# Weight sums of a seven-product unit: formed by accumulating transfers instead of VectorE, from quarter tiles

## The chip, the cores and the metric

The kernel runs on one core of a Trainium2 chip. The metric is the device time of one execution in microseconds. The engines are TensorE (PE in the profile), VectorE (DVE), ScalarE (ACT), GpSimd (POOL) and SyncE (SP); SP issues the loads from HBM, GpSimd issues a few transfers of its own queue.

## The reference

Two layers of a decoder trunk over 528 positions (16 meta and 512), with D = 1024 and FF = 2816, in fp32. Each layer is an FFN with a gate, a norm, a mixer, a norm, a second such FFN and a norm; the mixer is a short gated convolution in the first layer and forgetting attention in the second, whose K and V come from the end of the first.

```python
def swiglu(x, wg, wu, wd):
    return (jax.nn.silu(x @ wg) * (x @ wu)) @ wd
...
    for l in range(DEPTH):
        h = layer_norm(DEEPNORM_ALPHA * h + 0.5 * swiglu(h, ffn1_wg[l], ffn1_wu[l], ffn1_wd[l]),
                       ln_gain[l, 0], ln_bias[l, 0])
        if l < N_A:
            mix = short_conv(h, conv_w_in[l], conv_w[l], conv_w_out[l])
        else:
            j = l - N_A
            mix = forgetting_attention(h, attn_w_q[j], attn_w_o[j], k_sh, v_sh, c_sh)
        h = layer_norm(DEEPNORM_ALPHA * h + mix, ln_gain[l, 1], ln_bias[l, 1])
        h = layer_norm(DEEPNORM_ALPHA * h + 0.5 * swiglu(h, ffn2_wg[l], ffn2_wu[l], ffn2_wd[l]),
                       ln_gain[l, 2], ln_bias[l, 2])
        if l == N_A - 1:
            k_sh, v_sh, c_sh = shared_kv(h, kv_w, f_bias)
```

## The kernel before

Every fp32 matrix is used as a sum of a high and a low part. For a weight, ScalarE casts the raw tile to `wh` (L132) and VectorE subtracts to get `wl` (L134); this is `split_w`. A product is then three matmuls for one (`gemms`, L244): low times high, high times low, high times high.

The weights of gate and up (a pair `wg`, `wu`), and of K and V, are taken in **units** of 256 columns. A unit splits the 1024 rows of its weight and its 256 columns in two, so there are quarters a11, a12 (the upper rows), a21, a22 (the lower rows), each 128 x (2 matrices x 4 row blocks x 128 columns). In place of eight products of quarters it takes seven, with sums of weight quarters on the left and sums of activations (t1 to t4) on the right. The sums on the left are

- s1 = a21 + a22, s2 = s1 + a11, s3 = a11 + a21, s4 = s2 + a12 (signs are put into the activations).

In the kernel before, VectorE forms them: `s` into a tile of its own (L200), s3 in the place of a21 (L201), s2 in the place of a11 (L202), s4 in the place of a12 (L211). Each sum is then split like any weight. `Quads` holds the quarters of one unit; `Unit` holds the products p1 to p7; `run_units` sets TensorE's order: p5, p6, p7, the next unit's p1, then p4, p3, and the next unit's p2. Each product is 24 matmuls. p1 (a11), p6 (s2), p7 (s3) and p4 (a22) accumulate one after another into the same two PSUM banks (`pb`), and ScalarE copies the banks out after p1 (L544), p6 (L558) and p7 (L564); p5 (s1) and p3 (s4) go into two other banks. Where the first activations of an FFN are not ready in time for sums, its first unit is a `Direct` one: eight products of plain quarters.

There are 48 units: 11 in each of four FFNs, in chunks of 2, 3, 3 and 3, and 4 for K and V. Four are direct, so 44 form sums. After each chunk `down` multiplies the chunk's hidden rows with `wd` (`Weights`, loaded in pieces of 256 columns).

Raw weights lie in a pool of 3 tiles of 128 x 8 x 256 (L60); a unit takes two, one per half of the rows, each filled by two loads of 512 KB in runs of 1 KB. `wh` and `wl` have 5 tiles each, PSUM has 8 banks. TensorE's order is the one written out in the program. The other engines' order is made by the tile scheduler; each engine executes its queue in order, and a low part is placed right behind its cast (`behind`, L112). Among the steps around the change: `Mixed.early` (L312) prepares the left parts of a unit ahead of a norm's end; the norm's reciprocal root is a chain of small VectorE instructions (L351 to L359); `project` (calls at L1056) forms Q for some heads, for which `q_w` splits the weights.

Of the kernel before, what the change touches and what calls it, by code (L numbers as in the profile page):

```python
# [9 lines left out]
F32 = mybir.dt.float32  # L10
# [3 lines left out]
ALU = mybir.AluOpType  # L14
# [4 lines left out]
P = 128  # L19
D = 1024  # L20
KD = D // P
# [21 lines left out]
KH = KD // 2  # L43
# [3 lines left out]
def trunk_kernel(  # L47
# [7 lines left out]
    nc = tc.nc  # L55
# [15 lines left out]
    def htile(name, dtype=F32R):  # L71
        return hid.tile([P, T], dtype, tag="h", name=name)
# [38 lines left out]
    @contextmanager  # L111
    def behind(*after):  # L112


        with ExitStack() as stack:
            for ins in after or newest[-1:]:
                stack.enter_context(tc.issue_after(ins.ins))
            yield

    def split_w(src, shape, home=None):  # L120

        n = math.prod(shape)
# [12 lines left out]
        return a, b  # L135

    class Weights:


        def __init__(self, w_ap, r0, kn, c0, n):  # L140
            self.a, self.r0, self.kn, self.c0, self.n = w_ap, r0, kn, c0, n
            self.raw, self.got, self.home = {}, {}, {}

        def load(self, m):
            g = m // 2
            if g not in self.raw:
                raw = rawp.tile([P, KD, 256], F32, tag="raw", name="raw")
                self.raw[g] = raw
                c = self.c0 + g * 256
                nc.sync.dma_start(  # L150
                    raw[:, :self.kn, :],
                    self.a[self.r0:self.r0 + self.kn * P, c:c + 256].rearrange("(k p) n -> p k n", p=P))
            return self.raw[g]

        def __call__(self, m):
            if m not in self.got:
                raw = self.load(m)
                g = m - m % 2
                if self.kn <= KH:
                    src = raw[:, :self.kn, :].rearrange("p k (j n) -> p j k n", j=2)  # L160
                    wh, wl = split_w(src, (2, self.kn, P))
                    for j in range(2):
                        self.got[g + j] = wh[:, j], wl[:, j]
                else:
                    self.got[m] = split_w(
                        raw[:, :self.kn, (m - g) * P:(m - g + 1) * P], (self.kn, P), self.home.get(m))
            return self.got[m]

    class Quads:
# [1 line left out]

        def __init__(self, aps, home=None):
            self.aps, self.raws, self.got, self.home = aps, {}, {}, home

        def load(self, half):
            if half not in self.raws:
                raw = rawp.tile([P, KD, 256], F32, tag="raw", name="raw")
                raw = raw.rearrange("p (j k) n -> p j k n", j=2)  # L180
                self.raws[half] = raw
                for j, a in enumerate(self.aps):
                    nc.sync.dma_start(
                        raw[:, j], a[half * KH * P:(half + 1) * KH * P, :].rearrange(
                            "(k p) n -> p k n", p=P))
            return self.raws[half]

        def part(self, m, half):
            return self.load(half)[:, :, :, m * P:(m + 1) * P]

        def sums(self):
            if "s" in self.got:
                return
            self("a11")
            s = wp.tile([P, KD * P], F32, tag="ws", bufs=1, name="s")
            s = s.rearrange("p (j k n) -> p j k n", j=2, k=KH)
            self.got["s"] = s
            a11, a21, a22 = self.part(0, 0), self.part(1, 0), self.part(1, 1)
            with behind():
                nc.vector.tensor_tensor(s, a21, a22, ALU.add)  # L200
                nc.vector.tensor_tensor(a21, a11, a21, ALU.add)  # L201
                nc.vector.tensor_tensor(a11, a11, s, ALU.add)  # L202

        def __call__(self, name):
            if name not in self.got:
                if name[0] == "s":
                    self.sums()
                if name == "s4":
                    a12 = self.part(0, 1)
                    with behind():  # L210
                        nc.vector.tensor_tensor(a12, a12, self.part(0, 0), ALU.add)  # L211
                src = {"a11": lambda: self.part(0, 0), "a12": lambda: self.part(0, 1),
                       "a21": lambda: self.part(1, 0), "a22": lambda: self.part(1, 1), "s1": lambda: self.got["s"],
                       "s2": lambda: self.part(0, 0), "s3": lambda: self.part(1, 0),
                       "s4": lambda: self.part(0, 1)}[name]()
                self.got[name] = split_w(src, (2, KH, P), self.home)
            return self.got[name]


# [65 lines left out]
    class Mixed:  # L285
# [26 lines left out]
        def early(self):  # L312


            self.left("a11")
            self.left("a12")
            self.left.sums()

        def sums(self):

# [307 lines left out]
                nxt.p2()  # L628

    def pair_quads(wg, wu, c0, home=None):  # L630
        return Quads([a[:, c0:c0 + 256] for a in (wg, wu)], home)

    def ffn(layer, wg, wu, wd, ln, xs, to, last=None, ready=None, ahead=None):

# [58 lines left out]
    first = f1[0]  # L693
    half = D // 2
# [104 lines left out]
    def z_operands(h):  # L799
# [6 lines left out]
         Norm(0, 1, EPS, xs1), ALPHA, ahead=first_four(f2[0]))  # L806

    kv_quads = [
        Quads([kv_w[:, j * D + i * 256:j * D + (i + 1) * 256] for j in range(2)], None if i else xtile)
        for i in range(H // 2)]  # L810
    xs2 = Mixed(0, kv_quads[1])
    ffn(0, ffn2_wg[0], ffn2_wu[0], ffn2_wd[0], 2, xs1, xs2, ready=f2, ahead=first_four(kv_quads[0]))
# [353 lines left out]
```

## Time and profile before

| | |
|---|---|
| median of 3 runs | 1946.85 us (1944.77 to 1947.14) |
| the profiled execution | 1946.79 us, span 1945.0 us, mean granted clock 0.989 |
| TensorE busy | 1884.8 us, 97% |
| VectorE busy | 1404.0 us, 72% |
| ScalarE busy | 873.9 us, 45% |
| GpSimd busy | 136.7 us, 7% |
| load queue (q1) | 178510 packets, 182.74 MB, 29.3% of 16 engines |
| GpSimd's queue (q0) | 2016 packets, 5.49 MB, 0.8% |

The span is the time from the first to the last instruction; busy is the time in which an engine executes. TensorE is the engine that is nearly always busy, so what matters is where it stands still, and whom it waits for there. In the profile `pb`, `pc` and so on are PSUM banks named after the products, `wh`, `wl` the two parts of a weight, `xh`, `xl` and `hh`, `hl` those of activations, `s` the sum tile, `raw` the raw weights.

### The profile page before, as it was taken

What the parts mean: (1) busy time and instruction counts of PE and PEld (TensorE: products, weight loads), DVE (VectorE), ACT (ScalarE), POOL (GpSimd) and SP (SyncE); (2) the same over time, 40 slices, a digit from 0 to 9 for tenths busy, and PEclk for the clock granted to TensorE, in tenths of its full rate; (3) what the DMA queues carried; (4) which work ended last, traced back from release to release, by engine and by line L of the source; (5) the groups of instructions that cost most, each with busy time, mean ns of one, the idle gap of its engine ahead of it and who ended that gap; (6) DMA issues with size and microseconds to landing.
All of it is one profiled execution on the core that took longest, in us unless ns stands there. A gap on an engine that the chain in (4) does not pass through costs nothing.

```text
span 1945.0 us, 34609 instructions
## 1 busy us (share of the span) xinstructions
PE 1884.8 (97%) x14467; PEld 1820.9 (94%) x14467; DVE 1404.0 (72%) x2078; ACT 873.9 (45%) x1459; POOL 136.7 (7%) x198
## 2 busy tenths in 40 slices
PE   8899999999998999999999999999989989999997
PEld 7899999999998999999899998989988889989897
DVE  5785858674469776767887887767677787868685
ACT  5353535443335353535454543535455554535360
POOL 0000000300031000000411000000210220000000
PEclk9999999999999999999999999999989999999999
DMA  4333333232230332323224323232513203333241
GB/s 144 98 98 98 98 98 100 97 109 85 89 98 12 122 115 90 109 88 109 87 78 136 129 91 114 82 114 82 180 56 120 98 1 99 113 103 109 87 131 44
DMA packets 180681, 190.42 MB, mean 98 GB/s; under 512 B 5834, under 2 KB 174070, under 8 KB 180526
## 3 DMA queue, kind: packets, MB, share of 16 engines
q1 hardware_dynamic: 178510, 182.74, 29.3%
q0 software_dynamic: 2016, 5.49, 0.8%
q8 instruction: 113, 1.85, 0.4%
q14 instruction: 42, 0.34, 0.1%
HBM read 181.76 MB, written 6.44 MB: 97 GB/s over the span
## 4 chain that ended last, share of the span: by engine, by line
PE 84%; DVE 9%; DMA 2%; ACT 2%; POOL 1%; issue 1%; SPq 0%; DVEq 0%; ACTq 0%; POOLq 0%
PE pb L244 25%; PE pc L244 16%; PE pa L244 6%; PE pq L244 2%; PE pcc L244 2%; PE pcv L244 2%; PE pcb L244 2%; DVE wl L134 2%; DMA raw<-in_ffn_wu_dram 2%; PE psc L970 1%; PE po L1028 1%; DVE y L439 1%; POOL s L410 1%; ACT y L443 1%; POOL s L412 1%
## 5 line engine op out<-in xcount | busy, mean ns | idle before, releaser
L134 DVE TENSOR_TENSOR wl<-raw,wh 128x1024 fp32r<-128x1024 f32 (+1 forms) x440 | 522.1, 1192 | 196.5 <-ACT wh L132 185.0
L132 ACT CAST wh<-raw 128x1024 fp32r<-128x1024 f32 (+1 forms) x440 | 439.3, 1003 | 464.5 <-PE pc L244 74.9
L244 PE MATMUL pb<-xh,wl 128*128 128x264 f32 (+1 forms) x1408 | 398.1, 283 | 1.2 <-DVE wl L134 1.2
L244 PE MATMUL pb<-xh,wh 128*128 128x264 f32 (+1 forms) x1408 | 398.0, 283 | 0.0
L244 PE MATMUL pb<-xl,wh 128*128 128x264 f32 (+1 forms) x1408 | 397.8, 282 | 0.0
L244 PE MATMUL pc<-xh,wl 128*128 128x264 f32 (+1 forms) x960 | 276.4, 288 | 8.1 <-ACT xh L257 5.4
L244 PE MATMUL pc<-xl,wh 128*128 128x264 f32 (+1 forms) x960 | 276.0, 288 | 3.0 <-DVE xl L258 3.0
L244 PE MATMUL pc<-xh,wh 128*128 128x264 f32 (+1 forms) x960 | 275.1, 287 | 0.0
L244 PEld LDWEIGHTS pb<-xh,wl 128*128 128x128 f32 x1408 | 264.6, 188 | 1.6 <-issue 1.3
L244 PEld LDWEIGHTS pb<-xh,wh 128*128 128x128 f32 x1408 | 265.4, 189 | 0.0
L244 PEld LDWEIGHTS pb<-xl,wh 128*128 128x128 f32 x1408 | 264.5, 188 | 0.3
L244 PEld LDWEIGHTS pc<-xh,wl 128*128 128x128 f32 x960 | 184.2, 192 | 9.3 <-ACT xh L257 6.0
L244 PEld LDWEIGHTS pc<-xl,wh 128*128 128x128 f32 x960 | 184.2, 192 | 4.5 <-DVE xl L258 4.2
L244 PEld LDWEIGHTS pc<-xh,wh 128*128 128x128 f32 x960 | 184.7, 192 | 0.0
L244 PE MATMUL pa<-xh,wl 128*128 128x264 f32 (+1 forms) x352 | 99.6, 283 | 0.0
L244 PE MATMUL pa<-xh,wh 128*128 128x264 f32 (+1 forms) x352 | 99.5, 283 | 0.0
L244 PE MATMUL pa<-xl,wh 128*128 128x264 f32 (+1 forms) x352 | 99.4, 282 | 0.0
L132 ACT CAST wh<-s 128x1024 fp32r<-128x1024 f32 x44 | 46.0, 1046 | 49.0 <-DVE s L200 10.8
L244 PEld LDWEIGHTS pa<-xh,wh 128*128 128x128 f32 x352 | 66.3, 188 | 0.0
L244 PEld LDWEIGHTS pa<-xh,wl 128*128 128x128 f32 x352 | 66.1, 188 | 0.0
L244 PEld LDWEIGHTS pa<-xl,wh 128*128 128x128 f32 x352 | 66.1, 188 | 0.0
L200 DVE TENSOR_TENSOR s<-raw 128x1024 f32<-128x1024 f32 x44 | 54.2, 1232 | 15.5 <-DMA raw<-in_ffn_wu_dram 13.8
(1920 smaller groups left out, 4539.8 us busy)
## 6 DMA issues: line engine op xcount, KB each, us to landing
raw<-in_ffn_wg_dram SPq DMA_DIRECT2D x88, 512.0 KB, 3.9
raw<-in_ffn_wu_dram SPq DMA_DIRECT2D x88, 512.0 KB, 4.9
raw<-in_ffn_wd_dram SPq DMA_DIRECT2D x48, 768.0 KB, 4.6
raw<-in_conv_w_in_dram SPq DMA_DIRECT2D x12, 1024.0 KB, 4.9
raw<-in_ffn_wd_dram SPq DMA_DIRECT2D x16, 512.0 KB, 3.4
raw<-in_kv_w_dram SPq DMA_DIRECT2D x16, 512.0 KB, 4.6
raw<-in_conv_w_out_dram SPq DMA_DIRECT2D x4, 1024.0 KB, 5.4
raw<-in_attn_w_q_dram SPq DMA_DIRECT2D x4, 1024.0 KB, 4.8
```

The source lines that it names most:

```text
L132: nc.scalar.copy(a, src)
L134: nc.vector.tensor_tensor(b, src, a.bitcast(F32), ALU.subtract)
L200: nc.vector.tensor_tensor(s, a21, a22, ALU.add)
L244: nc.tensor.matmul(ps, lhsT=a[:, k, :], rhs=b(k), start=start and k == ks[0] and j == 0, stop=stop and k == ks[-1] and j == 2, skip_group_ ...
L410: nc.gpsimd.tensor_tensor(self.s1[h], yv[:, 0, :] if m == 1 else self.s1[h], yv[:, m, :], ALU.add)
L412: nc.gpsimd.tensor_tensor(self.s2[h], self.s2[h], sq, ALU.add)
L439: nc.vector.tensor_tensor(ym, ym, rb, ALU.mult)
L443: nc.scalar.activation(yv[:, j, :], yv[:, j, :], AF.Identity, scale=vecs[:, c:c + 1], bias=vecs[:, 48 + c:49 + c])
L970: nc.tensor.matmul(ps, lhsT=q[:, M + t * P:M + (t + 1) * P], rhs=kt[:, a:b], start=True, stop=True)
L1028: nc.tensor.matmul(po[:, q0:S], lhsT=vt[:, j * P:(j + 1) * P], rhs=pT[j // 2][:, j % 2, q0:S], start=j == 0, stop=False)
```

## The change

- Raw weights lie in 7 tiles of half the size. Each quarter of a unit has a tile of its own, filled by two loads of 256 KB (one per matrix) in runs of 512 B.
- The sums are no longer formed by VectorE, but by transfers of GpSimd's queue that read a quarter from HBM a second time and add it to what lies in a tile (`accum_op`). s1's tile gets a21 by a load, then a22 is added. Once s1 is split, a11 is added in the same tile: s2. Once s2 is split, a12 is added: s4. The tile of a11, once split, gets a21 added: s3. That is four pairs of added transfers per unit, 352 in all.
- `Weights` whose pieces have over 4 row blocks are loaded in single column blocks of 128 (runs of 512 B) rather than two at a time.
- `early` no longer forms sums; direct units load plain quarters; in the start two quarters are loaded before the rest of x.
- Q's first two batches are 2 and 3 heads, not 3 and 2.

The core of the diff:

```diff
-    rawp = ctx.enter_context(tc.tile_pool(name="rawp", bufs=3))
+    rawp = ctx.enter_context(tc.tile_pool(name="rawp", bufs=7))
...
+    def raw_tile(*shape):
+
+        raw = rawp.tile([P, KH * 2 * P], F32, tag="raw", name="raw")[:, :math.prod(shape)]
...
     class Weights:
...
+            self.step = 2 if kn <= KH else 1
...
     class Quads:
...
-            with behind():
-                nc.vector.tensor_tensor(s, a21, a22, ALU.add)
-                nc.vector.tensor_tensor(a21, a11, a21, ALU.add)
-                nc.vector.tensor_tensor(a11, a11, s, ALU.add)
+        NEXT = {"a11": ("s3", "a21"), "s1": ("s2", "a11"), "s2": ("s4", "a12")}
...
+        def move(self, engine, dst, name, **kw):
+            m, half = int(name[1]) - 1, int(name[2]) - 1
+            for j, a in enumerate(self.aps):
+                engine.dma_start(
+                    dst[:, j], a[half * KH * P:(half + 1) * KH * P, m * P:(m + 1) * P].rearrange(
+                        "(k p) n -> p k n", p=P), **kw)
+
+        def raw(self, name):
+            if name not in self.raws:
+                t = raw_tile(2, KH, P)
+                self.move(nc.sync, t, "a21" if name == "s1" else name)
+                if name == "s1":
+                    self.move(nc.gpsimd, t, "a22", accum_op=ALU.add)
+                self.raws[name] = t
+            return self.raws[name]
...
         def __call__(self, name):
             if name not in self.got:
...
+                t = self.raw(name)
+                self.got[name] = split_w(t, (2, KH, P), self.home)
+                if name in self.NEXT and not self.direct:
+                    then, part = self.NEXT[name]
+                    self.move(nc.gpsimd, t, part, accum_op=ALU.add)
+                    self.raws[then] = t
             return self.got[name]
...
             self.left("a11")
             self.left("a12")
-            self.left.sums()
...
-            first.load(0)
-    first.load(1)
+            first.raw("a11")
+            first.raw("a21")
+    first.load()
...
-    project(range(3), [0])
-    project(range(3, 5), [0])
+    project(range(2), [0])
+    project(range(2, 5), [0])
```

What this does to the order of the engines is shown at three places. First ScalarE, in the third unit of the second chunk of the first FFN; before, the rows run from the cast of s2 to the eviction of p6 (`pb_2282`, `pb_2283`).

```order
L132 CAST wh<-raw 128x1024 [waits Activation_49]
L649 ACTIVATE g<-pb_2112 128x264 [waits PE_49]
L132 CAST wh<-raw 128x1024 [waits PE_49,Activation_49]
L257 CAST hh<-g 128x528 [waits DVE_49]
L655 ACTIVATE g<-g 128x528 [waits DVE_49]
L132 CAST wh<-raw 128x1024 [waits DMAHW0_49,DMAHW1_49,PE_49,Activation_49]
L257 CAST hh<-g 128x528 [waits DVE_49]
L132 CAST wh<-raw 128x1024 [waits PE_49,Activation_49] x2
L558 COPY g<-pb_2282 128x264 [waits PE_49]
L558 COPY u<-pb_2283 128x264 [waits PE_49]
```

In the changed kernel the same stretch, from the cast of s2 to the eviction of p6 (`pb_2339`, `pb_2340`), reads as follows; DMASW are semaphores of GpSimd's queue, DMAHW those of SP's loads.

```order
L132 CAST wh<-raw 128x1024 [waits DMASW4_49,DMASW3_49,Activation_49]
L257 CAST hh<-g 128x528 [waits DVE_49]
L132 CAST wh<-raw 128x1024 [waits DMASW0_49,DMASW7_49,PE_49,Activation_49]
L654 ACTIVATE g<-g 128x528 [waits DVE_49]
L132 CAST wh<-raw 128x1024 [waits DMAHW6_49,DMAHW7_49,PE_49,Activation_49]
L257 CAST hh<-g 128x528 [waits DVE_49]
L132 CAST wh<-raw 128x1024 [waits DMAHW0_49,DMAHW1_49,PE_49,Activation_49]
L132 CAST wh<-raw 128x1024 [waits DMASW5_49,DMASW6_49,PE_49,Activation_49]
L557 COPY g<-pb_2339 128x264 [waits PE_49]
L557 COPY u<-pb_2340 128x264 [waits PE_49]
```

The sequence of casts and copies is nearly the same; s2, s3 and s4 (the rows with DMASW) now wait for transfers of GpSimd's queue, and s4's cast stands right ahead of p6's eviction, as it did before.

Second GpSimd. Before, its queue goes from the transfers of the start (L711, L859) straight to the sums of the first norm; in all FFN units it has nothing.

```order
L710 DMA vr<-in_conv_w_dram 24x128
L711 DMA fbias<-in_f_bias_dram 8x1
L859 DMA fr<-in_kv_w_dram 128x8x8
L765 MEMSET us 128x2 [waits DVE_49]
L410 TENSOR_TENSOR s_4035<-y 128x264 [waits DVE_49]
L410 TENSOR_TENSOR s_4035<-s_4035,y 128x264 [waits DVE_49,Pool_49]
```

In the changed kernel it has eight rows for each unit. Those from one unit's s3 to the next unit's read in this way; L191 is `Quads.move`, rows with DVE wait for a low part or for a free tile.

```order
L191 DMA raw<-in_ffn_wg_dram 128x4x128 [waits DMAHW6_49,DMASW7_49,DVE_49]
L191 DMA raw<-in_ffn_wu_dram 128x4x128 [waits DMAHW7_49,DMASW0_49]
L191 DMA raw<-in_ffn_wg_dram 128x4x128 [waits DMASW6_49,DMASW5_49,DMAHW4_49,DMASW1_49,DVE_49]
L191 DMA raw<-in_ffn_wu_dram 128x4x128 [waits DMAHW5_49,DMASW2_49]
L191 DMA raw<-in_ffn_wg_dram 128x4x128 [waits DVE_49]
L191 DMA raw<-in_ffn_wu_dram 128x4x128
L191 DMA raw<-in_ffn_wg_dram 128x4x128 [waits DMASW3_49,DVE_49]
L191 DMA raw<-in_ffn_wu_dram 128x4x128 [waits DMASW4_49]
L191 DMA raw<-in_ffn_wg_dram 128x4x128 [waits DMAHW2_49,DMAHW3_49,DMASW7_49,DMAHW6_49,DVE_49,Activation_49]
L191 DMA raw<-in_ffn_wu_dram 128x4x128 [waits DMAHW7_49,DMASW0_49]
```

What moved: four sums a unit from VectorE's queue to this one, where each pair waits for the split of what the tile held.

Third VectorE, in the last part of the second norm of the first layer (after the convolution). Before, the sum s of the next unit stands between two low parts and the last addition to the residual, `y<-y,pd__6553`.

```order
L258 TENSOR_TENSOR xl<-y,xh 128x528 [waits DVE_49,Activation_49] x2
L134 TENSOR_TENSOR wl<-raw,wh 128x1024 [waits DMAHW5_49,DMAHW4_49]
L134 TENSOR_TENSOR wl<-raw,wh 128x1024 [waits DMAHW7_49,DMAHW6_49]
L200 TENSOR_TENSOR s<-raw 128x1024
L501 TENSOR_TENSOR y<-y,pd__6553 128x264 [waits PE_49]
L201 TENSOR_TENSOR raw<-raw 128x8x128 [waits DVE_49]
L202 TENSOR_TENSOR raw<-raw,s 128x8x128 [waits DVE_49]
```

In the changed kernel the same place has the same addition under the name `pd__6709`, and behind it the norm's own chain.

```order
L258 TENSOR_TENSOR xl<-y,xh 128x528 [waits DVE_49,Activation_49] x2
L134 TENSOR_TENSOR wl<-raw,wh 128x1024 [waits DMAHW1_49,DMAHW0_49]
L134 TENSOR_TENSOR wl<-raw,wh 128x1024 [waits DMAHW3_49,DMAHW2_49]
L500 TENSOR_TENSOR y<-y,pd__6709 128x264 [waits PE_49]
L430 SCALAR_TENSOR_TENSOR v<-pv,v 128x264 [waits PE_49,Activation_49]
```

The two low parts stay ahead of the addition; the three sums around it are gone.

## Rows read from the trace of the kernel before

**Rows 1.** Page, busy time: engine, busy us (share of the span), instructions.
```profile
PE 1884.8 (97%) x14467; PEld 1820.9 (94%) x14467; DVE 1404.0 (72%) x2078; ACT 873.9 (45%) x1459; POOL 136.7 (7%) x198
```

**Rows 2.** Windows, unit stretch: start:end length, busy us by engine, granted clock, DMA share, GB/s.
```profile
100.00:300.00 200.00, 200.00 (x1650) 200.00 (x1649) 140.11 (x186) 87.24 (x128) 0.00 (x0) 1.00 0.32 101
```

**Rows 3.** Waits of PE: who waited <- for whom: us in total, times, longest.
```profile
PE pq L244 <- DVE wl L134: 5.5, 1, 5.5
PE pd L420 <- DVE y L501: 5.5, 2, 5.3
PE pc L244 <- ACT xh L257: 5.4, 3, 2.3
...
PE pd__783 L244 <- ACT hh L257: 2.8, 1, 2.8
PE pc L244 <- DVE wl L134: 2.8, 1, 2.8
...
PE pb L244 <- DVE wl L134: 1.2, 1, 1.2
```

**Rows 4.** Tile raw, whole span: line, engine, operation, count: ns min/median/max, first and last start.
```profile
L183 SPq DMA_DIRECT2D raw<-in_ffn_wg_dram x88: 367/368/402, 3.5 to 1857.4; - x88
...
L200 DVE TENSOR_TENSOR s<-raw x44: 1206/1220/1756, 39.8 to 1863.0; 128x1024 f32<-128x1024 f32 x44
```

**Rows 5.** Chain, window 196 to 240: start us, us, what.
```profile
202.57 11.61 PE pb L244 x96
...
222.91 11.61 PE pb L244 x96
```

**Rows 6.** Timeline of ACT, one unit: start us, us, line, operation, idle before and its releaser.
```profile
208.99 1.05 ACT L132 CAST wh<-s 128x1024 fp32r<-128x1024 f32 x1
...
211.58 1.05 ACT L132 CAST wh<-raw 128x1024 fp32r<-128x1024 f32 x1
...
223.01 1.05 ACT L132 CAST wh<-raw 128x1024 fp32r<-128x1024 f32 x1 [1.85 <-PE pc L244]
224.40 0.38 ACT L558 COPY g<-pb 128x264 f32<-128x264 f32 x1 [0.34 <-PE pb L244]
```

**Rows 7.** Timeline of DVE, the same unit.
```profile
210.35 1.22 DVE L134 TENSOR_TENSOR wl<-s,wh 128x1024 fp32r<-128x1024 f32 x1
```

**Rows 8.** Timeline of DVE, norm after the convolution.
```profile
588.37 3.44 DVE L134 TENSOR_TENSOR wl<-raw,wh 128x1024 fp32r<-128x1024 f32 x2
591.74 1.76 DVE L200 TENSOR_TENSOR s<-raw 128x1024 f32<-128x1024 f32 x1
593.42 0.41 DVE L501 TENSOR_TENSOR y<-y,pd__6553 128x264 f32<-128x264 f32 x1
```

**Rows 9.** Chain, window 960 to 985.
```profile
967.26 1.13 DVE s L200
...
970.08 1.14 DVE raw L202
```

**Rows 10.** Timeline of ACT, 69 to 80 us.
```profile
72.90 1.04 ACT L132 CAST wh<-raw 128x1024 fp32r<-128x1024 f32 x1 [3.23 <-DMA raw<-in_ffn_wu_dram]
73.85 0.63 ACT L257 CAST hh<-g 128x528 fp32r<-128x528 f32 x1
```

**Rows 11.** DMA issues, whole span: out<-in, engine, count, KB each, median us to landing.
```profile
raw<-in_ffn_wg_dram SPq DMA_DIRECT2D x88, 512.0 KB, 3.9
raw<-in_ffn_wu_dram SPq DMA_DIRECT2D x88, 512.0 KB, 4.9
...
v_dram<-vk POOLq DMA_DIRECT2D x8, 256.0 KB, 2.9
```

**Rows 12.** Lines 825 and 859: POOL's DMA issues, columns as for the tile raw.
```profile
L825 POOL DMA_DIRECT2D v_dram<-vk x8: 539/550/580, 998.3 to 1070.5; - x8
...
L859 POOL DMA_DIRECT2D fr<-in_kv_w_dram x1: 957/957/957, 4.1 to 4.1; - x1
```

**Rows 13.** Page, DMA queues: packets, MB, share of 16 engines.
```profile
q1 hardware_dynamic: 178510, 182.74, 29.3%
```

More of the change, by code (lines that the diff above doesn't have):

```diff
@@ L135, in split_w @@
         return a, b
+    def raw_tile(*shape):
+        raw = rawp.tile([P, KH * 2 * P], F32, tag="raw", name="raw")[:, :math.prod(shape)]
+        if len(shape) == 3:
+            return raw.rearrange("p (j k n) -> p j k n", j=shape[0], k=shape[1])
+        return raw.rearrange("p (k n) -> p k n", k=shape[0])
     class Weights:
@@ L141, in __init__ @@
             self.a, self.r0, self.kn, self.c0, self.n = w_ap, r0, kn, c0, n
+            self.step = 2 if kn <= KH else 1
             self.raw, self.got, self.home = {}, {}, {}
         def load(self, m):
-            g = m // 2
+            g = m - m % self.step
             if g not in self.raw:
-                raw = rawp.tile([P, KD, 256], F32, tag="raw", name="raw")
-                self.raw[g] = raw
-                c = self.c0 + g * 256
+                n = self.step * P
+                self.raw[g] = raw_tile(self.kn, n)
+                c = self.c0 + g * P
                 nc.sync.dma_start(
-                    raw[:, :self.kn, :],
-                    self.a[self.r0:self.r0 + self.kn * P, c:c + 256].rearrange("(k p) n -> p k n", p=P))
+                    self.raw[g],
+                    self.a[self.r0:self.r0 + self.kn * P, c:c + n].rearrange("(k p) n -> p k n", p=P))
             return self.raw[g]
@@ L157, in __call__ @@
                 raw = self.load(m)
[L158 to L161, printed above, removed]
+                if self.step == 2:
+                    wh, wl = split_w(raw.rearrange("p k (j n) -> p j k n", j=2), (2, self.kn, P))
                     for j in range(2):
-                        self.got[g + j] = wh[:, j], wl[:, j]
+                        self.got[m - m % 2 + j] = wh[:, j], wl[:, j]
@@ L164, in __call__ @@
                 else:
-                    self.got[m] = split_w(
-                        raw[:, :self.kn, (m - g) * P:(m - g + 1) * P], (self.kn, P), self.home.get(m))
+                    self.got[m] = split_w(raw, (self.kn, P), self.home.get(m))
             return self.got[m]
     class Quads:
[L174 to L198, printed above, removed]
-            with behind():
-                nc.vector.tensor_tensor(s, a21, a22, ALU.add)
-                nc.vector.tensor_tensor(a21, a11, a21, ALU.add)
-                nc.vector.tensor_tensor(a11, a11, s, ALU.add)
+        NEXT = {"a11": ("s3", "a21"), "s1": ("s2", "a11"), "s2": ("s4", "a12")}
@@ new lines, in __init__ @@
+        def __init__(self, aps, home=None, direct=False):
+            self.aps, self.home, self.direct = aps, home, direct
+            self.raws, self.got = {}, {}
+        def move(self, engine, dst, name, **kw):
[4 more added lines that the diff above has]
+                        "(k p) n -> p k n", p=P), **kw)
@@ new lines, in raw, with load @@
+        def raw(self, name):
[6 more added lines that the diff above has]
+            return self.raws[name]
+        def load(self):
+            for name in ("a11", "a21", "a12", "a22") if self.direct else ("a11", "a12", "s1", "a22"):
+                self.raw(name)
@@ L204, in __call__ @@
         def __call__(self, name):
             if name not in self.got:
[L206 to L215, printed above, removed]
@@ L216, in __call__ @@
-                self.got[name] = split_w(src, (2, KH, P), self.home)
+                t = self.raw(name)
[4 more added lines that the diff above has]
+                    self.raws[then] = t
             return self.got[name]
@@ L630, in pair_quads @@
     def pair_quads(wg, wu, c0, home=None):
-        return Quads([a[:, c0:c0 + 256] for a in (wg, wu)], home)
+        return Quads([a[:, c0:c0 + 256] for a in (wg, wu)], home, home is not None)
     def ffn(layer, wg, wu, wd, ln, xs, to, last=None, ready=None, ahead=None):
@@ L808, in trunk_kernel @@
     kv_quads = [
-        Quads([kv_w[:, j * D + i * 256:j * D + (i + 1) * 256] for j in range(2)], None if i else xtile)
+        Quads([kv_w[:, j * D + i * 256:j * D + (i + 1) * 256] for j in range(2)], None if i else xtile, i == 0)
         for i in range(H // 2)]
```

## The prediction

> **What bounds the kernel now.** I read the table of busy times first, then windows by stage, then TensorE's waits, then one steady unit line by line. TensorE is busy for 97% of the span, VectorE for 72% [rows 1]: VectorE's sums can only matter where TensorE stands. In the unit stretch from 100 to 300 us TensorE is busy for all of the 200 us at full granted clock, while DMA is used at 0.32 [rows 2]. All waits of TensorE together are 48 us, in the start and around the norms; the six that this change can touch are shown [rows 3]. So of the 215 us of VectorE sums (44 units, 4 adds of 1.22 us, the first of them in [rows 4]) the part hidden under a busy TensorE gives nothing back.
>
> In a steady unit the 96 matmuls on the `pb` banks (s2's product p6, p7, the next unit's p1, p4) take 11.61 us, begin at 202.57 and again at 222.91 [rows 5]: one unit per 20.34 us, and 2.90 us for a product of 24. ScalarE is in order, and its queue in such a unit is casts and evictions mixed: s1's cast at 208.99, s2's at 211.58, s4's at 223.01, right behind it the eviction of p6's first bank at 224.40 [rows 6]. VectorE ends s1's low part at 211.57 [rows 7]. TensorE needs that first bank again for p7 at 222.91 + 2.90 = 225.8, since p7 accumulates into it.
>
> **What the change removes.** All 176 adds of VectorE, and the wait of each sum for both halves' loads. Where do they stand on a path that TensorE waits for?
> - At 593.89 TensorE had waited 5.3 us for `y<-y,pd__6553` [rows 3]. Ahead of it on VectorE stand two low parts (3.44 us) and one sum of 1.76 us [rows 8]. The order of the changed kernel keeps the two low parts and drops the sum: 1.7 us.
> - In the norm at 967 three sums of 1.13 to 1.14 us stand inside the rsqrt chain, on the chain of waits [rows 9], 3.4 us; the same stands once more, around 1581. TensorE's wait for `xh` behind the two is at most 2.3 us each (three times, 5.4 us) [rows 3], so I take 2 us each: 4 us.
> - `pq` waited 5.5 us once for a low part [rows 3]. Q's first batch is now two heads, not three; these two have their own tiles, and 48 matmuls (5.8 us at 2.90 per 24) run before the third is needed: 5 us.
> - `pd__783` waited 2.8 us [rows 3], because ScalarE stood at a cast of a raw tile whose load was late [rows 10]. Seven quarter tiles come free sooner than three halves; half of it, 1.4 us.
> Sum: about 12 us. Bounds: 0 (another instruction is late in each place: one more cast or low part is queued in all of them) and 20 (the whole of the 5.3 us, and the 2.8 and 1.2 us for low parts in the start, [rows 3]).
>
> **What it adds.** Per unit four pairs of accumulating transfers of 256 KB on GpSimd's queue, 352 transfers, 92 MB more of HBM reads. Loads get runs of 512 B for 1 KB: twice the packets. Loads stay ahead of their use by the seven tiles; I cost them at nothing as long as the DMA engines have room (0.32 now). Their issues on SP nearly double, at some 0.37 us each [rows 4], on an engine that does nothing else: nothing.
>
> The real price is a chain that did not exist. s2 is s1 + a11, formed in s1's own tile, and s4 is s2 + a12 in the same tile. So: s1's cast and low part must end, then a pair lands (time D from GpSimd's issue to landing), then s2's cast and low part (1.05 + 1.22 + 0.1), then another pair, then s4's cast. Before, s2 and s4 cost VectorE 1.22 us each and were there before ScalarE asked. Now, from [rows 7]: s2 is there at 211.6 + D; its low part ends at 214.0 + D; s4 is there at 214.0 + 2D. s4's cast (1.05) and the eviction behind it (0.38) must be over at 225.8, so the cast must begin by 224.35. It follows that **2D must not exceed 10.3: D up to 5.15 us costs nothing, and each us beyond costs 2 us a unit**, since ScalarE, waiting in order at s4's cast, holds p6's eviction and with it TensorE. (s2 itself is needed at 222.9, so its own limit is D = 8.9, and the casts that queue behind s2's still fit: three casts of 1.05 and three smaller pieces of 0.65, 5.1 us of work from 218.6.)
>
> This holds where a unit follows a unit. A unit that comes first after a down phase has that phase's time. Tight are two units in each of three chunks of four FFNs (24), one in the first chunk of the FFN without a direct unit, and two of K/V: 27.
>
> **D.** No accumulating transfer is in the trace, so by bounds. Low: 3.5, a 256 KB store from GpSimd lands in 2.9 us [rows 11], plus the pair's second issue of 0.55 [rows 12]. High: 9.8, a `wg`/`wu` load twice (4.9 each, [rows 11]), if the reads of both operands come one after the other or the queue is shared with the next unit's pair. Nearest row: a `wg`/`wu` pair of plain loads, which has the same 512 packets per transfer, and moves as many bytes as an accumulating pair reads in all (512 KB from HBM and 512 KB from SBUF). Its second lands 4.9 after its issue, which is 0.4 after the first's: 5.3. GpSimd issues more slowly, 0.55 for a store and 0.96 for the transfer of 128x8 short runs [rows 12], against SP's 0.37: 0.5 more for two. With a little for the third unit's pair that stands just ahead on the same queue I take D = 6.0. The loss is 27 x 2 x (6.0 - 5.15) = 46 us, the net 46 - 12 = +34.
>
> The Trainium skill has a rule that speaks for the other side. Its page "Collectives: The Full Stack" (Part 3, the bandwidth ceiling) says that an add in the DMA engine is slow only because it reads two sources, one descriptor each, so it goes at half a copy's rate. From rows: the second load of a pair lands 1.0 us later than the first, so 512 KB of plain data are 1.0 us and a fixed part is 2.9; two accumulations of 256 KB at half rate are 2.0, D is then 4.9 to 5.2 with GpSimd's issues, at the limit and not beyond it. That is the first rival. No run here shows an add so far.
>
> The profiled execution lasted 1946.8 us (span 1945.0), the median of the runs 1946.85, so sums against either are the same. **Forecast: 1946.8 + 34 = 1981 us.** With D from 5.5 to 7.5 (loss 19 to 127) this case alone reaches from 1954 to 2062.
>
> **Rivals.**
> - *In time* (D up to about 5.2): no wait in the units, the gains of 12 stand, up to 20: 1927 to 1943, best 1935. For it: the DMA engines are idle two thirds of the time, and the rule above. Against it: it has to hold twice in a row, with GpSimd's issues and the loads' doubled packets beside it.
> - *DMA engines fill up*: the 178510 packets of the load queue are 29.3% of 16 engines [rows 13], 51 ns for a packet of mostly 1 KB. A unit now has 4096 packets of loads and 4096 of accumulation; if a 512 B packet with an add still takes 51 ns, they need 8192 x 51 / 16 = 26 us, more than the 20.34 of a unit. Then D is 8 and more and raw tiles are late as well; from 8 on the loss is 27 x 5.7 = 154: 2090 us, with 26 - 20.3 on each of 44 units on top 2180 or more. It decides from 40 ns a packet. Against it: packets of half the size should take less, the two-thirds idle.
> - *Nothing moves*: D just over the limit, so that 12 us of waits come back as 12 us of stalls (D = 5.4), or the gains at the norms are eaten by other late instructions while D is short: 1943 to 1951.
>
> **Chances.** A run can tell 0.2% from no change here, 3.9 us. Late sums 0.46 (0.43 slower, 0.03 the same), in time 0.33 (0.32 faster, 0.01 the same), engines full 0.12 (slower), nothing moves 0.09 (0.07 the same, 0.02 slower). In all faster 0.32, the same 0.11, slower 0.57. The range goes from 1930, the in-time case with nearly all gains, to 2110, the lower end of the full engines; the rest of that case is left out.
>
> **What would show it.** Right: in the unit stretch ScalarE's casts of `raw` wait for an accumulating transfer, TensorE's matmuls on `pb` wait for the evictions of p6 (`u` and `g` copies) one after another in every second and third unit of a chunk, 1 to 2 us each; issue to landing of the accumulating transfers near 5 to 6 us; VectorE busy near 1190. The `pq` wait and the sums in the rsqrt chain gone. Wrong: a TensorE row without waits from 100 to 300 us and landing times under 4.5 (the first rival), or a DMA share over 0.9 in the units with late loads from SP (the second). Wrong in size: stalls in first units too, or a p5 that waits because s1 itself, now behind a load and an accumulation, comes late.

## The result and the profile after

The changed kernel takes 2250.41 us (median of 4 runs, 2242.2 to 2261.14) against 1946.99 us: 1.156 times as long (95% interval 1.151 to 1.161), 303 us more. The forecast said slower by this mechanism, 1981 us, with a range up to 2110: the sign and the place were right, the size was not. Two runs below had one execution each at a far lower granted clock (0.56 and 0.73); their medians leave it out.

The page's table of busy times for the changed kernel answers to [rows 1].

```profile
PE 1967.0 (88%) x14467; PEld 1891.9 (84%) x14467; DVE 1202.8 (54%) x1902; ACT 856.5 (38%) x1459; POOL 584.2 (26%) x550
```

VectorE gave up 201 us, as it should, and no one gained by it. TensorE was idle for 60 us of the span before (1945.0 - 1884.8), now for 281 (2247.7 - 1967.0): 220 of the 303 us. The other 82 us are TensorE's own busy time, which rose with the same instructions. TensorE's waits for others, answering to [rows 3], show the first part.

```profile
PE pb L244 <- ACT g L557: 206.1, 37, 8.9
PE pb L244 <- ACT kT L557: 9.6, 3, 4.3
PE pb L244 <- DVE wl L134: 8.1, 7, 2.0
PE pb L244 <- ACT u L557: 7.3, 1, 7.3
PE pd L419 <- DVE y L500: 4.3, 3, 4.0
```

L557 is the eviction of p6. Three rows of the five wait for it, 223 us, once in each of 41 of the 44 units with sums. The waits that the forecast wanted gone are gone or less: `pq` (5.5) and `pd__783` (2.8) are not in the list any more, `pd` for `y` fell from 5.5 to 4.3, `pc` for `xh` from 5.4 to 1.0: 13.9 us, for the 12 that I had summed. Some 15 us of other waits are new or longer: for low parts on `pb` (8.1 for 1.2), and around K and V (`pc` 4.2, `pvt` 2.8 and 1.2).

One unit shows how the wait comes about. The first rows are GpSimd's timeline, the next VectorE's and the third ScalarE's (start, duration, instruction, idle time before it and its releaser); the last is TensorE's.

```profile
209.61 1.26 POOL L191 DMA_DIRECT2D raw<-in_ffn_wg_dram  x1 [5.36 <-DVE y L504]
...
234.90 1.26 POOL L191 DMA_DIRECT2D raw<-in_ffn_wg_dram  x1 [10.34 <-DMA raw<-in_ffn_wg_dram]
235.65 1.82 POOL L191 DMA_DIRECT2D raw<-in_ffn_wu_dram  x1
236.40 2.38 POOL L191 DMA_DIRECT2D raw<-in_ffn_wg_dram  x1
...
247.27 1.27 POOL L191 DMA_DIRECT2D raw<-in_ffn_wg_dram  x1 [7.18 <-DVE wl L134]
```

```profile
234.04 1.23 DVE L134 TENSOR_TENSOR wl<-raw,wh 128x1024 fp32r<-128x1024 f32 x1 [0.29 <-ACT wh L132]
...
245.75 1.23 DVE L134 TENSOR_TENSOR wl<-raw,wh 128x1024 fp32r<-128x1024 f32 x1 [5.65 <-ACT wh L132]
```

```profile
244.67 1.05 ACT L132 CAST wh<-raw 128x1024 fp32r<-128x1024 f32 x1 [7.53 <-DMA raw<-in_ffn_wu_dram]
...
249.13 1.05 ACT L132 CAST wh<-raw 128x1024 fp32r<-128x1024 f32 x1
255.43 1.04 ACT L132 CAST wh<-raw 128x1024 fp32r<-128x1024 f32 x1 [5.25 <-DMA raw<-in_ffn_wu_dram]
256.38 0.37 ACT L557 COPY g<-pb 128x264 f32<-128x264 f32 x1
```

```profile
256.81 0.59 PE L244 MATMUL pb<-xh,wl 128*128 128x264 f32 x1 [6.61 <-ACT g L557]
```

s1's low part ends at 235.27 (234.04 + 1.23). GpSimd has just sent the next unit's pair for s1 (234.90, 235.65), so s2's pair goes out at 236.40 and is there at 244.67, when ScalarE's cast begins: 9.4 us from the low part's end, 8.3 from the issue. s2's low part ends at 246.98; s4's pair goes out at 247.27 and is there at 255.43, 8.2 us later. ScalarE stood at s4's cast for 5.25 us with p6's eviction right behind it, and TensorE waited 6.61 us for that eviction. In the kernel before, s4's cast began 11.4 us after s1's low part [rows 6, 7], now 20.2.

Why is TensorE's busy time up? Windows of that unit, and as the last row the whole unit stretch, with the columns of [rows 2]:

```profile
243.00:252.00 9.00, 7.06 (x57) 6.64 (x55) 6.25 (x9) 5.51 (x7) 2.57 (x2) 1.00 0.47 59
252.00:262.00 10.00, 5.19 (x23) 5.19 (x24) 4.13 (x5) 2.93 (x5) 2.57 (x2) 0.53 1.09 214
256.80:259.00 2.20, 2.19 (x10) 2.19 (x11) 1.92 (x2) 1.18 (x2) 0.00 (x0) 0.50 1.40 185
263.00:266.00 3.00, 3.00 (x27) 3.00 (x26) 1.99 (x3) 1.88 (x4) 0.00 (x0) 1.00 0.01 2
100.00:300.00 200.00, 171.90 (x1340) 170.65 (x1339) 96.40 (x138) 75.74 (x118) 51.98 (x41) 0.92 0.72 135
```

In the second row, which takes in the end of the wait and the 5 us behind it, the mean granted clock is 0.53. Right behind the wait, in which TensorE had stood for 6.61 us, it is 0.50, the lower of its two levels, 1.2 GHz: 10 matmuls take 2.2 us there, where from 263 us on, at 1.00, 27 take 3.0. Groups of instructions say the same over the whole run: a `pb` matmul, the one behind such waits, takes 304 to 312 ns for 283 before; a `pc` one 286 to 288, as before. 82 us over 41 waits are 2.0 us for each, on top of the wait.

The transfers on the queues (packets, MB, share of 16 engines; then count, KB, median us to landing) answer to [rows 11, 13]:

```profile
q0 software_dynamic: 187872, 97.78, 34.3%
q1 hardware_dynamic: 342478, 182.75, 28.6%
...
raw<-in_ffn_wg_dram POOLq DMA_DIRECT2D x164, 256.0 KB, 5.4
raw<-in_ffn_wu_dram POOLq DMA_DIRECT2D x164, 256.0 KB, 7.4
```

The load queue has twice the packets and the same share of the engines. An added packet of some 520 B costs 66 ns of an engine (0.343 x 16 x 2247.7 us / 187872), a loaded one of 534 B 30 ns. With the second transfer issued 0.75 us after the first and landing 7.4 us later, D is 8.2 at the median; pair by pair, one in ten takes under 6.9 and one in ten over 10.4.

Two sentences of the description of the kernel before have to be put right: `behind` holds the low parts and sums behind the last VectorE instruction of a norm, not behind their cast; and a11 and a21 are the quarters of the upper rows, a12 and a22 those of the lower. No term of the sum rested on either.

### The profile page after: what moved, and what is told of

It reads as the page before. It is cut to its first block, busy times and chain, and to the rows that moved or that the text cites. A ratio compares the mean times of both kernels' runs of the same rounds, so it can differ in the third digit from the quotient of the medians.

```text
span 2247.7 us, 36078 instructions
## 1 busy us (share of the span) xinstructions
PE 1967.0 (88%) x14467; PEld 1891.9 (84%) x14467; DVE 1202.8 (54%) x1902; ACT 856.5 (38%) x1459; POOL 584.2 (26%) x550
## 3 DMA queue, kind: packets, MB, share of 16 engines
q0 software_dynamic: 187872, 97.78, 34.3%
q1 hardware_dynamic: 342478, 182.75, 28.6%
## 5 line engine op out<-in xcount | busy, mean ns | idle before, releaser
L134 DVE TENSOR_TENSOR wl<-raw,wh 128x1024 fp32r<-128x1024 f32 (+1 forms) x484 | 567.9, 1185 | 472.7 <-ACT wh L132 464.9
L132 ACT CAST wh<-raw 128x1024 fp32r<-128x1024 f32 (+1 forms) x484 | 481.1, 1006 | 827.4 <-DMA raw<-in_ffn_wu_dram 543.2
L244 PE MATMUL pb<-xh,wl 128*128 128x264 f32 (+1 forms) x1408 | 439.0, 312 | 231.3 <-ACT g L557 206.1
L191 POOL DMA_DIRECT2D raw<-in_ffn_wg_dram x164 | 223.4, 1375 | 1179.2 <-DVE wl L134 632.7
L244 PEld LDWEIGHTS pb<-xh,wl 128*128 128x128 f32 x1408 | 299.3, 213 | 242.0 <-ACT g L557 214.2
L244 PE MATMUL pb<-xl,wh 128*128 128x264 f32 (+1 forms) x1408 | 430.1, 305 | 0.0
L244 PE MATMUL pb<-xh,wh 128*128 128x264 f32 (+1 forms) x1408 | 428.6, 304 | 0.0
L191 POOL DMA_DIRECT2D raw<-in_ffn_wu_dram x164 | 311.1, 1953 | 0.0
L244 PEld LDWEIGHTS pb<-xl,wh 128*128 128x128 f32 x1408 | 299.6, 213 | 0.3
L244 PEld LDWEIGHTS pb<-xh,wh 128*128 128x128 f32 x1408 | 298.4, 212 | 0.0
```

The source lines that it names most:

```text
L191: engine.dma_start(dst[:, j], a[half * KH * P:(half + 1) * KH * P, m * P:(m + 1) * P].rearrange("(k p) n -> p k n", p=P), **kw)
L244: nc.tensor.matmul(ps, lhsT=a[:, k, :], rhs=b(k), start=start and k == ks[0] and j == 0, stop=stop and k == ks[-1] and j == 2, skip_group_ ...
```

## The experiments

**The add left out.** All transfers of GpSimd's queue stay, but overwrite.

```diff
-                    self.move(nc.gpsimd, t, part, accum_op=ALU.add)
+                    self.move(nc.gpsimd, t, part)
```

> The changed kernel with the same transfers on GpSimd's queue, but each overwrites its tile instead of adding to it, so the sums are left out. In the changed kernel a pair takes 8.2 us from issue to landing, the second transfer landing 2.7 us behind the first (86 ns per 512 B packet and engine). Theory 1 (the add itself, with its second read in the DMA engine, sets that rate): the second transfer of a pair lands about 1.0 to 1.4 us behind the first, a pair takes 5 to 5.5 us, and of the 231 us of waits for p6's evictions under 30 stay; time 1950 to 1980. Theory 2 (GpSimd's software queue is slow, 1.3 and 1.8 us per issue against SP's 0.37): the pair takes 7.5 us or more without the add as well, and the time stays over 2180. Theory 3 (the DMA engines are too full): time over 2100, because the loads of 512 B runs are all still there.

1943.92 us in its one run, beside 1945.52 for the kernel before and 6 us under the range of Theory 1. TensorE's first wait, and the queue:

```profile
PE pb L244 <- ACT g L557: 10.4, 9, 2.5
```

```profile
q0 software_dynamic: 30176, 97.78, 16.3%
...
raw<-in_ffn_wg_dram POOLq DMA_DIRECT2D x164, 256.0 KB, 3.3
raw<-in_ffn_wu_dram POOLq DMA_DIRECT2D x164, 256.0 KB, 3.7
```

The pair now takes 0.75 + 3.7 = 4.45 us, under the limit of 5.15, and the waits for p6 fall from 223 us (the 231 of the expectation hold the waits for low parts too) to 12 (the row and 1.9 us for `u`). So the bytes from HBM, the loads' doubled packets and GpSimd's queue as such are not the cost; what the add brings is, through D. One caution: without the add the same bytes travel in 30176 packets, not 187872, and an issue takes 0.75 us for 1.26 to 1.82 (the second of a pair begins 0.75 us after the first either way). The engines' share over 100 to 300 us falls with it, from 0.72 to 0.55. The run takes away the second read, the small packets, the long issue and a good part of the engines' load together, so by itself it does not tell a late chain from full engines; the runs with fewer adds below do.

**s4's cast moved on ScalarE**, behind the evictions of the next unit's p1.

```diff
             u.p4()
+            with behind((nxt or u).last):
+                u.quads("s4")
             u.p3()
```

> The changed kernel with s4's cast placed behind the evictions of the next unit's p1 on ScalarE, in place of ahead of p6's evictions; the transfers are the same. Theory (ScalarE, waiting in order at s4's cast, holds p6's eviction and with it TensorE): the waits of TensorE for the copies of p6 fall from 231 us to under 50, since s4 is then needed only 8.7 us later (for p3); the clock goes back to 0.98 or more; time 1950 to 2010. Rival (a unit's chain of load, pair, split, pair, split is itself longer than 20.3 us, or the queue is): the wait only moves, TensorE waits for s4's low part at p3 or for s2's at p6 for about as long, time over 2150.

2166.25 us, 1.113 times before (1.111 to 1.116). The waits of TensorE:

```profile
PE pb L244 <- DVE wl L134: 119.7, 30, 6.0
PE pc L244 <- DVE wl L134: 37.5, 18, 4.2
```

The wait for p6's eviction is gone, which shows that it was ScalarE's order that held TensorE. But what came next was late too: s2's low part for p6 (`pb`) and s4's for p3 (`pc`). Of the 303 us, 84 went; I had expected 240 or more, and the rival was right about the rest. The eviction was only the first thing in TensorE's way behind a chain that is itself too long.

**The queue's order as well**: the next unit's s1 pair behind this unit's s2 pair.

```diff
-                    self.move(nc.gpsimd, t, "a22", accum_op=ALU.add)
+                    with behind(*Quads.pair[-1:]) if Quads.pair else ExitStack():
+                        self.move(nc.gpsimd, t, "a22", accum_op=ALU.add)
```

> The changed kernel with s4's cast behind the evictions of the next p1 (as in the run before) and in addition, on GpSimd's queue, the next unit's s1 pair behind this unit's s2 pair in place of ahead of it. Latency alone (a pair of 8.2 us instead of 9.4 to 10 with another pair ahead): s2 is there in time for p6, waits under 30 us, 1950 to 1965. Throughput of the queue (eight added transfers of 2.7 us are 21.9 us per unit, more than the 20.34 that TensorE needs): the waits stay at 1.6 us a unit or more, 70 us in all, wherever they show; 2000 to 2090. If the order of the queue does nothing: 2166 as before.

2133.64 us, 1.097 times before (1.093 to 1.100), some 33 us under the run before. It does a little, but neither figure that I expected. Nothing here shows its waits, so what bounds this version stays open.

**s4 by VectorE**: one link of the chain taken out.

```diff
-        NEXT = {"a11": ("s3", "a21"), "s1": ("s2", "a11"), "s2": ("s4", "a12")}
+        NEXT = {"a11": ("s3", "a21"), "s1": ("s2", "a11")}
...
+                if name == "s4":
+                    t = self.raws["a12"]
+                    with behind():
+                        nc.vector.tensor_tensor(t, t, self.raws["s2"], ALU.add)
+                    self.raws["s4"] = t
```

> The changed kernel, but s4 is added by VectorE in a12's tile (one add of 1.22 us per unit, 44 in all); s1, s2 and s3 are accumulated as before. Theory: the second link of the chain goes, s4 is there about 1.2 us after s2 and well ahead of its cast, so only s2's own limit (8.9 us for its pair) is left; waits for p6's evictions under 40 us, time 1945 to 1990. Rival (the queue's throughput or late loads bound a unit): a quarter less work on the queue gives back only about a quarter of the loss, 2150 to 2200.

2027.0 us, 1.041 (1.040 to 1.043): a quarter of the added transfers gone, and 223 of the 303 us. That speaks for the chain and against a cost by traffic or by full engines, whose share over 100 to 300 us is the same as in the changed kernel, 0.72. But 37 us more stay than I allowed. TensorE's first waits and the window:

```profile
PE pb L249 <- DVE wl L134: 21.8, 14, 4.7
PE pb L249 <- ACT g L562: 19.6, 20, 3.0
```

```profile
100.00:300.00 200.00, 194.83 (x1589) 193.24 (x1588) 111.31 (x161) 81.28 (x125) 46.45 (x36) 1.00 0.72 141
```

The first are waits at p6 for s2's low part, the second for p6's evictions (L562 here): s2 is late by both. ScalarE's timeline shows how that reaches the eviction.

```profile
224.22 1.05 ACT L132 CAST wh<-raw 128x1024 fp32r<-128x1024 f32 x1 [7.88 <-DMA raw<-in_ffn_wu_dram]
225.17 0.63 ACT L262 CAST hh<-g 128x528 fp32r<-128x528 f32 x1
225.71 1.04 ACT L132 CAST wh<-raw 128x1024 fp32r<-128x1024 f32 x1
226.66 0.64 ACT L659 ACTIVATE g<-g 128x528 f32<-128x528 f32 x1
227.20 1.03 ACT L132 CAST wh<-raw 128x1024 fp32r<-128x1024 f32 x1
228.52 0.64 ACT L262 CAST hh<-g 128x528 fp32r<-128x528 f32 x1 [0.29 <-DVE g L660]
229.06 1.99 ACT L132 CAST wh<-raw 128x1024 fp32r<-128x1024 f32 x2
230.96 0.37 ACT L562 COPY g<-pb 128x264 f32<-128x264 f32 x1
```

From s2's cast to p6's eviction ScalarE has 6.74 us of work without a gap to speak of. The eviction must begin by 225.4 in the times of [rows 6] (225.8 - 0.38), so s2's cast by 218.7, and s2's own limit is D = 7.1 (218.7 - 211.6), not the 8.9 at which TensorE needs s2.

**Only s1 and s3 accumulated**, s2 and s4 by VectorE.

```diff
+                if name == "s1":
+                    self("a11")
+                    t, a11 = self.raws["s1"], self.raws["a11"]
+                    with behind():
+                        nc.vector.tensor_tensor(t, t, a11, ALU.add)
+                    self.raws["s2"] = t
+                    self.move(nc.gpsimd, a11, "a21", accum_op=ALU.add)
+                    self.raws["s3"] = a11
```

> The changed kernel with s1 and s3 accumulated, s2 and s4 added by VectorE (88 adds of 1.22 us), so no accumulated sum waits for the split of another; half the traffic of the queue stays. Theory (the price is the chain: accumulated sums whose input is itself a late sum): waits for p6's evictions under 10 us, 1935 to 1950. Rival (adding transfers cost by slowing the loads and the queue, half the traffic is a third to a half of the loss): over 1980.

2038.74 us, 1.046 (1.044 to 1.049). My number was wrong by 90 us, and by its number the rival holds. The trace gives another reason than its traffic: in this edit s3 may only be added once VectorE has read a11 for s2. GpSimd's row and the two of ScalarE:

```profile
216.09 1.27 POOL L190 DMA_DIRECT2D raw<-in_ffn_wg_dram  x1 [1.53 <-DVE raw L220]
```

```profile
224.17 1.05 ACT L132 CAST wh<-raw 128x1024 fp32r<-128x1024 f32 x1 [4.97 <-DMA raw<-in_ffn_wu_dram]
...
230.11 0.37 ACT L564 COPY g<-pb 128x264 f32<-128x264 f32 x1
```

The pair waits for VectorE's add (L220) and takes 8.1 us, though the engines' share over 100 to 300 us is down to 0.59, and ScalarE holds everything behind s3's cast. I had moved one late pair to another sum, not removed it. So a single pair of 8 us in the middle of a unit is enough for 80 to 90 us; two in series make 303. Whether half the traffic off the path would be free is not settled by this run.

**The layout alone**: quarter tiles, loads of 512 B runs, single column blocks and the order of Q, with all sums on VectorE.

```diff
-    rawp = ctx.enter_context(tc.tile_pool(name="rawp", bufs=7))
+    rawp = ctx.enter_context(tc.tile_pool(name="rawp", bufs=6))
...
+            s = wp.tile([P, KD * P], F32, tag="ws", bufs=1, name="s")
...
+                nc.vector.tensor_tensor(s, a21, a22, ALU.add)
+                nc.vector.tensor_tensor(a21, a11, a21, ALU.add)
+                nc.vector.tensor_tensor(a11, a11, s, ALU.add)
```

> The layout alone: quarter tiles (six of them and the old tile for s), loads of 512 B runs and single column blocks as in the changed kernel, but all sums on VectorE. Theory (the layout costs nothing, all of the loss is the accumulation): within 1% of before, 1935 to 1965. Rival (twice the packets make raw tiles late and take a share of the loss): over 1980, with casts that wait for loads.

1934.98 us, 0.9947 (0.9931 to 0.9964). It beats both kernels: everything in the change but the accumulation is a gain of 10.5 us, and the doubled packets cost nothing that shows.

Two runs split that gain. **With the three sums back ahead of a norm's end** (`self.left.sums()` in `early`):

> Quarter tiles with all sums on VectorE (as the run that gave 1935), but with the three sums back in the part prepared ahead of a norm's end, as in the kernel before. If the sums inside the norm's chain were worth the 1.7 and 4 us that I put on them: 1939 to 1942. If quarter tiles and the order of Q's heads are all of the gain: 1935.

1944.29 us, 0.9982 (0.9973 to 0.9992): against the 0.9947 of the run before, 0.35% or 7 us of the gain are the sums that leave the norm's chain (10 us against its repeat below), where I had 5.7. TensorE waits there as before:

```profile
PE pc L257 <- ACT xh L270: 6.3, 3, 3.0
PE pd L433 <- DVE y L514: 5.5, 2, 5.3
```

**The kernel before with only the order edits** (no sums ahead of a norm's end, Q's heads 2 and 3):

> The kernel before with its half tiles and VectorE sums, with two edits of the change alone: no sums ahead of a norm's end, and Q's first batches of 2 and 3 heads. By my terms (5 for Q, 4 + 1.7 for the norms): 1934 to 1937. If the gain came from quarter tiles instead: 1943 to 1947.

1938.94 us, 0.9956 (0.9941 to 0.9971), 9.9 us under its kernel before, for the 10.7 of my terms: nearly all of the gain is in these two edits. Quarter and half tiles once more, side by side:

> Quarter tiles with all sums on VectorE once more, on the same chip as the half tiles with the same order. If quarter tiles themselves are worth something (I put 1.4 us on loads that come in time): 1 to 4 us below the half tiles; if the whole gain is the order of the sums and of Q's heads: the same within 1 us.

> Half tiles, VectorE sums, no sums ahead of a norm's end, Q's batches of 2 and 3 heads, once more: 0.4 to 0.6% under the kernel before, 1936 to 1941.

Quarter tiles 1934.18 us, 0.9931 (0.9916 to 0.9947); half tiles 1939.32 us, 0.9950 (0.9933 to 0.9967). The quarter tiles were the faster both times, by 0.09% and 0.19% of the kernel before (2 and 4 us), but the intervals overlap: a sign, not shown.

**The transfers by themselves.** A first run ran its kinds into one another:

> Transfers of 256 KB alone, eight in a row of each kind, with nothing computed (the whole network is left out): added ones of 512 B, 1 KB and 2 KB runs and from SBUF, plain ones on GpSimd's queue and on SP's, and added ones beside plain loads. In the kernel an added transfer lands 2.7 us behind the one before it. Theory A (an added 512 B packet costs this by itself): 2.4 to 2.9 us apart with nothing beside it, plain ones 0.7 to 1.0. Theory B (contention with the doubled loads): under 1.6 us apart alone, and over 2.2 beside plain loads. If the price is by packet, runs of 1 KB halve it (1.3); if by byte, they leave it at 2.7.

It gave no clean rates, and was repeated with VectorE reading all eight tiles (`wait`) and writing them (`again`) before the next kind.

```diff
+    for i in range(n):
+        nc.gpsimd.dma_start(v(t[i], 4), quarter(ffn1_wg, i), accum_op=ALU.add)
+    wait()
+    again()
```

> Transfers of 256 KB alone (the whole network is left out), each kind for itself, since in the first such run the kinds ran into one another: a pair of added ones of 512 B runs; then eight in a row of: added 512 B runs, plain on GpSimd's queue, added 1 KB, added 2 KB, plain on SP; then eight added beside eight plain ones of SP. Read per kind: the first landing, and the last minus the first over seven. Theory A (the add is slow by itself): the lone pair takes 7 to 8.2 us and adds of 512 B land 2.0 to 2.7 us apart, plain ones 0.7 to 1.0. Theory B (only the neighbours make it slow): the lone pair under 5.5 us, adds under 1.4 apart, and over 2.2 beside SP's loads. Price by packet: 1 KB runs land about half as far apart; price by byte: the same distance.

The kinds' lines, each with its issues (duration in ns, first and last start) and its landing times: eight added, eight plain on GpSimd's queue, eight added of 2 KB runs, eight added beside SP's loads, and these loads.

```profile
L91 POOL DMA_DIRECT2D t<-in_ffn_wg_dram x8: 1283/3248/5216, 21.0 to 26.3; - x8
...
DMA to landing us min/median/max: 4.5/7.7/10.1
```

```profile
L95 POOL DMA_DIRECT2D t<-in_ffn_wu_dram x8: 754/756/778, 39.8 to 45.0; - x8
...
DMA to landing us min/median/max: 3.4/4.2/4.9
```

```profile
L103 POOL DMA_DIRECT2D t<-in_ffn_wu_dram x8: 885/1733/2418, 72.8 to 77.5; - x8
...
DMA to landing us min/median/max: 4.0/7.4/9.4
```

```profile
L113 POOL DMA_DIRECT2D t<-in_ffn_wd_dram x8: 1298/2686/4653, 104.4 to 113.1; - x8
...
DMA to landing us min/median/max: 4.9/10.5/15.2
```

```profile
L114 SPq DMA_DIRECT2D u<-in_ffn_wd_dram x8: 368/1014/2386, 108.4 to 116.0; - x8
...
DMA to landing us min/median/max: 5.1/10.6/13.2
```

Taking the shortest landing as the first transfer's and the longest as the last's: added ones land (26.3 + 10.1 - 21.0 - 4.5) / 7 = 1.56 us apart alone, plain ones 0.96, added ones of 2 KB runs 1.44. Beside SP's loads the longest landing is not the last's; the last lands 13.6 us after its issue, so (113.1 + 13.6 - 104.4 - 4.9) / 7 = 2.5. So neither theory was right as put: alone an add costs 1.6 times a copy, nearly by byte and not by packet, and beside plain loads added ones land 1.6 times further apart again.

The trace shows what the neighbours do. Once both kinds are under way, they land by turns, one added and one plain every 2.6 us, about the 1.56 and the 0.96 that they take alone. So the engines serve both, and an added transfer waits for the loads served between. (In the kernel the medians to landing put a pair's second transfer 2.7 us behind its first; pair by pair the median is 2.25.)

The lone pair was not one: its second transfer waited, and each landed 4.5 us after its issue. Of the eight added ones the second, issued 0.75 us after the first, takes 6.0 to its landing: D = 6.75 with no neighbour but the six behind it.

## Why the prediction was wrong

- *The path* was right: the chain s1, s2, s4 through the tile, ScalarE in order at s4's cast, p6's eviction behind it, TensorE at p7. All of it is in the unit above, and moving the cast (2166 us) took away just that wait. The gains (12 forecast, 13.9 in the waits, 10.5 in the run with the layout alone) were right too.
- *D* failed, the term that carries the loss. I took 6.0; in the kernel it is 8.2, and 9.4 from the low part's end where the next unit's pair stands ahead. I priced a pair as a plain pair of 512 KB loads (5.3), with 0.5 for GpSimd and "a little" for neighbours. Two things were too small. The add itself: 6.75 with no loads beside it, already past the limit of 5.15, where the same pairs without the add take 4.45 in the kernel. And the neighbours: loads are served between the added transfers, which I take for the other 1.4 us of the median. By the formula this unit would lose 9.4 + 8.45 (s2's low part to s4's cast) - 10.3 = 7.5 us; it lost 6.61.
- *The count* failed: 27 units were to be tight, 41 waited. By the times of the waits, nine of the 14 more are first units of a chunk and three stand behind a direct unit, so the down phase gives a first unit less than I took for granted. In the first unit of this chunk a pair went out at 209.61 only, after GpSimd had stood idle for 5.36 us until VectorE released it; for the others this is not shown.
- *The clock* was put at nothing: 2.0 us for each wait of 5.4, 82 in all. Short waits did not cost it: with s4 on VectorE the waits from 100 to 300 us are of 1.2 us at most, and the granted clock of that stretch is 1.00.
- *s2's limit* of 8.9 was TensorE's; ScalarE's queue behind s2's cast sets it at 7.1.

The three sizes together: 41 units by 5.4 us of wait (223 us) and 2.0 us of clock (82), less the gains of 13.9 and with the 15 of other waits, 306 for the 303 measured. With the forecast's formula and D = 8.8 (the mean of 9.4 and 8.2) alone it would have been 27 x 7.3 = 197.

The rivals. *In time* is refuted here (D over 8). Its D of 4.9 came of a slip in reading the rows: the second load takes 1.0 us longer from its own issue, 0.4 after the first's, so it lands 1.4 later, not 1.0, and the same steps give 2.5 + 2.8 = 5.3, past the limit before GpSimd's issues are added. The rule that it leaned on, half a copy's rate (the Trainium skill, "Collectives: The Full Stack", Part 3), agrees roughly with the spacing of the adds alone, 1.6 times a copy's.

*Full engines* is refuted as the cause, but not as a part. The time is that case's, and so are the packets: 66 and 30 ns are 48 in the mean, over the 40 at which it was to decide. Packets overlap on the engines, though (a share of 1.09 in the window in which s4's pair travels), so this is not engine time; by the 2.6 us for an added and a plain transfer together, a unit's eight of each need 20.8 us, close to TensorE's 20.34. Against it as the cause: the share over 100 to 300 us is 0.72, under the 0.9 that it asked for, and stays 0.72 with s4 on VectorE, where 223 of the 303 us are gone; SP's loads land in 4.1 to 4.4 us (2.9 to 3.3 with the layout alone); and TensorE's waits name one eviction. What the busy engines do is make D long. Whether they also bound the two runs with s4's cast moved, at some 25 us a unit (20.34 and a 44th of what those runs lose), is open.

## What to carry to other kernels

An add of 1.2 us that hides under a busy TensorE was not worth trading for a transfer here: the transfer has an issue-to-landing time, and two that depend on one another put it on the path twice. Ask of each new wait how long the engine that waits in order has work queued behind it, and who needs that work; the limit can be set by that queue before it is set by the consumer of the late operand. Price a transfer beside the traffic that it will have as a neighbour, and add the clock's loss to long stalls of TensorE (2.0 us for one of 5.4 here).

## What the runs showed of the hardware

- An accumulating transfer of 256 KB from HBM into SBUF lands 1.56 us behind the one before, a plain one 0.96. Runs of 2 KB for 512 B change this little (1.44). Beside plain loads the two land by turns, one of each every 2.6 us.
- A pair of accumulating transfers takes 6.75 us from the first issue to the second landing with no loads beside it, 8.2 at the median in the kernel, 4.45 there without the add.
- The same transfers without the add travel in 30176 packets for 187872, and GpSimd's issue takes 0.75 us for 1.26 to 1.82; the second issue of a pair begins 0.75 us after the first in both.
- Halving the runs of SP's loads from 1 KB to 512 B doubled their packets (178510 to 342478) and left their share of the engines at 28.6% of a longer span, 32.4% with the layout alone for 29.3%.
- After TensorE had stood for 6.61 us the granted clock was 0.50, the lower of its two levels (1.2 GHz); over a stretch with seven waits of up to 1.2 us it was 1.00.
